# Narrow side products in the full shape of the array, and attention scores of both halves of the partitions in turns

## The chip, the cores and the metric

The kernel runs on one core of a Trainium2 chip. The metric is device time in microseconds (us) for one execution of the whole program; a lower time is better. The tensor engine (PE) multiplies, the vector engine (DVE) and the scalar engine (ACT) work on its results, GpSimd (POOL) and SyncE (SP) mainly start transfers (DMA).

## The reference

Two blocks of two layers each work on `x` of 256 tokens and 1024 channels, in float32. What the change touches is in the lines below: in the first block the retention with its normalisation by head, in the second the indexer of the sparse attention, the gates of the mLSTM, the norms of queries and keys, and the two attentions with a softmax (sparse attention over the keys that the indexer chose, and the difference of two softmax maps, weighted by lambda).

```python
# first block
o = head_groupnorm(retention_chunkwise(qh, kh, vh))
y_ret = (silu(g_ret) * o) @ w_ret_out
...
# second block: indexer and sparse attention
rel = relu(einsum('bqhd,bsd->bqhs', qi, ki))
score = einsum('bqh,bqhs->bqs', wi * idx_scale, rel)
_, idx = top_k(where(causal, score, -inf), 64)
p = softmax(einsum('bqhd,bqkhd->bhqk', q, k_sel) * dh ** -0.5)
y_b = einsum('bhqk,bqkhd->bqhd', p, v_sel)
...
# differential attention
lam_val = exp(sum(lam[0] * lam[1])) - exp(sum(lam[2] * lam[3])) + lam_init
p = softmax(einsum('bqhcd,bshcd->bhcqs', dq, dk) * d ** -0.5)
y_c = einsum('bhqs,bshv->bqhv', p[:, :, 0] - lam_val * p[:, :, 1], dv)
```

Around these stand the large products with the weights (`w_in`, the branches' matrices, the feed-forward matrices), which make up nearly all of the arithmetic.

## The kernel before

**Main products.** The weights come from memory in one stream of chunks, in the order in which PE takes them. ACT rounds each chunk to a high part `whi`, DVE forms the rest `wlo`; the activations are split in the same way (`hh` and `hl`, `yh` and `yl`). A 128x128 block of weights then meets 256 tokens in three products, `whi` with `hh`, `whi` with `hl` and `wlo` with `hh`, which add up in a PSUM tile `acc` (method `job`, through the helper `mm`, L403).

**Side products.** Everything else on PE goes to PSUM tiles named `sp`, of which there are four buffers: sums over channels by a table of constants, scores, transpositions (helper `tr`, L408), products of probabilities and values. They are written in Python generators, which `job` advances between its main products. The framework's scheduler then fixes one order for each engine, and every engine takes its own order strictly from the front. A visit, below, is a run of side products between two main products.

**Shapes of a side product.** The constants `cst` hold tables: `st4` (the mean over a head of 128 channels, one of four columns filled), `st8` (over 64 channels, eight columns), `hm2`, and `sel`, which picks the rows of `misc` that hold the mLSTM's gates. Multiplied with a table of 4 or 8 columns PE uses 4 or 8 columns of the array; with 64 rows of `misc` or with scores, whose channels are 64, half of its rows; with the gate rows `rows` four rows; with lambda (`lnl`) one row. Profile rows give this as `128*4`, `64*128`, `4*128`, `1*128`, and the full array as `128*128`. These products are in float32 and run in two passes each; the trace has one record for each pass. A transposition by `tr` has one.

**Scores.** Channels of 64 mean that a tile of 128 partitions holds two heads, or two maps, one in each half of the partitions. The work goes by groups of sets in the same half. There are two query tiles `t` of 128 tokens; tile 0 sees 128 keys, with four sets in a group, tile 1 sees 256 keys, with two. In the generator `ahead` each group is scored into one `sp` tile, masked by DVE into `prob`, its row maxima `smx` are reduced on DVE, and ACT takes the exponential with the row sums (`softmax_group`). One group is kept ahead of its use; its use is `transposed` (four transpositions of `prob` into `sp`, which ACT copies to `pt`) and a product of `pt` with the values `sv` or `dv`, into `yt`. For differential attention two maps are joined before the transposition.

**What stands ahead on the queues.** SP carries the weight stream and the rows that go to many partitions (`spread`); POOL carries exchanges of channels for the rotation (`swap`) and rows that go to DRAM (`rows`).

Of the kernel before, what the change touches and what calls it, by code (L numbers as in the profile page):

```python
# [29 lines left out]
TAKEN = -3.4e38  # L30

# [15 lines left out]
# norms after which the first chunks of weights and what they meet go unsplit  # L47
WHOLE = (1, 2, 3, 4)
# tiles of a product that ends a chain, the last ones apart
COLUMNS = ((0, 2), (2, 2), (4, 2), (6, 1), (7, 1))  # L50
# gates and products of the branches, in their order
# [8 lines left out]
def ffn_up(arr, l):  # L60
    """Gate and value tiles side by side; the first two products take four tiles."""
    t = [[_cols(i * P, P), _cols(FF + i * P, P)] for i in range(KF)]
    return [(arr, (l,), "B", KD, c) for c in [t[0] + t[1], t[2] + t[3]] + t[4:]]


def plan():
    """The weights in the order in which the tensor engine takes them: (array, index, kind,
    k tiles, columns), kind "B" by column tiles of 128 and "A" by rows of 512."""
# [104 lines left out]
def pack_params(inputs=None):  # L173
    """Per-channel parameters, channels on partitions: (offsets, array)."""
# [38 lines left out]
def make_consts():  # L213
    """Tables that depend on shapes alone: (offsets, array [128, n])."""
# [12 lines left out]

    add("ident", np.eye(P))
# [8 lines left out]
    e4 = np.zeros((P, 4, 4))  # L237
    for h in range(4):
        e4[:, h, h] = 1.0 / P
    add("st4", e4)  # L240
    s8 = np.zeros((P, 4, 8))
    for t in range(4):
        s8[:64, t, 2 * t] = 1.0 / 64
        s8[64:, t, 2 * t + 1] = 1.0 / 64
    add("st8", s8)
    hm = np.zeros((P, 2))
    hm[:64, 0] = 1.0 / 64
    hm[64:, 1] = 1.0 / 64
    add("hm2", hm)
    sel = np.zeros((P, 3, 4))  # L250
    for h in range(4):
        sel[64 + h, 0, h] = 1.0
        sel[68 + h, 1, h] = 1.0
        sel[72 + h, 2, h] = 1.0 / 16
    add("sel", sel)
# [15 lines left out]
def whole_chunks():  # L271
    """The chunks that go to the tensor engine as float32, unsplit."""
    out, n, i = set(), 0, 0
    for _, _, kind, nk, cols in plan():
        if kind == "B" and len(cols) == 4:
            if i // 2 in WHOLE:
                out.add(n // CB)
            i += 1
        n += nk * (len(cols) if kind == "B" else 4)
    return out  # L280


class Weights:
    """The stream of weights: loads ahead, then each chunk as the sum of two float32r parts."""
# [13 lines left out]
    def cuts(self, c):  # L298
        """The first chunk comes in halves."""
        return [slice(0, CW // 2), slice(CW // 2, CW)] if c == 0 else [slice(0, CW)]  # L300
# [43 lines left out]
class Gen:  # L344
# [44 lines left out]

    def p(self, name, l, i=0, n=1):  # L390
        o, m = self.poff[(name, l)]
        assert i + n <= m
        return self.prm[:, o + i:o + i + n]
# [53 lines left out]
    def split(self, hi, lo, src):  # L447
        """src as the sum of its float32r rounding and of the exact rest."""
# [3 lines left out]
    def behind(self, engine):  # L452
        """What is traced here is issued after the engine's last urgent instruction."""
# [21 lines left out]
    def side(self):  # L475
        """Steps of the tasks beside the products, as far as the vector engine keeps up."""
# [13 lines left out]
    def job(self, evac, mov, needs=(), scale=None, last=False, spare=None):  # L490
        """The next product of the plan. mov(k) gives the two parts of the activations' tile k;
        scale, per token, is for activations that were not normalised yet; spare gives tiles."""
# [3 lines left out]
        if kind == "B":  # L496
            n = len(cols)
            accs = [self.acc() for _ in range(-(-n // 2))]
            if self.idle is not None:
                # only to keep the tensor engine's clock up while it waits  # L500
# [4 lines left out]
            for k in range(nk):  # L505
                xs = mov(k)
                for t in range(n):
# [4 lines left out]
                    # a start clears the marks of its whole bank: the first product of a bank has it  # L512
# [32 lines left out]
    def swap(self, out, src):  # L545
        """src with the halves of each 64 channels exchanged"""
# [3 lines left out]
    def rows(self, r):  # L550
        # r in DRAM, from where a row goes to many partitions
# [4 lines left out]
    def spread(self, out, row):  # L556
        """a row on all the partitions of out"""
        self.nc.sync.dma_start(out, row.to_broadcast(list(out.shape)))

# [7 lines left out]
    def _lam(self, pool):  # L567
# [14 lines left out]
        ps = self.sp()  # L582
        self.mm(ps[:, 0:2], self.ones[0:1, 0:P], nl)
        self.copy(self.nlam, ps[:, 0:2])
# [6 lines left out]
    def rstd(self, pool, ps, scale, name):  # L591
        """1 / sqrt(scale * ps + eps)"""
# [6 lines left out]
    def sumsq(self, out, last, hold):  # L599
        """Over channels, on every partition: the sum of the squares of the eight tiles, which it  # L600
        takes by pairs, the last two also one by one (send). The first ones are added up before.
        With hold the tensor engine gets them together at the end."""
# [37 lines left out]
    def start_norm(self, g, l, folded=4):  # L640
        """Takes x by pairs of tiles (feed) for a norm whose scale per token comes last."""
# [20 lines left out]
    def end_norm(self, sd=None):  # L662
        """What the first products take, with their scale, and what the others take."""
# [38 lines left out]
    def branches(self, order, bufs, pool, mov, gate_load, needs, ys, done):  # L702
        """The sum over branches of gate * (branch output times its matrix), as two parts. A gate
        sigmoid(z) comes as tanh(z / 2), its double less 1."""
# [57 lines left out]
    def unscale(self, sd):  # L762
        """x out of u"""
# [10 lines left out]
    def out_proj(self, mov, g, l):  # L774
        """Four products whose columns are scaled by g, with the sum of their squares."""
# [11 lines left out]
    def first_mix(self, l, norm):  # L787
        dmov, rs, whole, mov = norm
        nc = self.nc
        with ExitStack() as st:  # L790
# [6 lines left out]
            def new_y(b):  # L797
                """Buffers for a branch's output, once those of the one before last are free."""
# [13 lines left out]
            # conformer convolution  # L812
# [65 lines left out]
            # retention  # L878
# [18 lines left out]
            def ret_a():  # L897
# [10 lines left out]
                for h in range(4):  # L908
                    ps = self.sp()
                    t, b = h // 2, (h % 2) * 64  # L910
                    q, k = rot["q"][b:b + 64, t], rot["k"][b:b + 64, t]
                    self.mm(ps[:, :T], k[:, :P], q)
                    self.mm(ps[:, T:T + P], k[:, P:], q[:, P:])
                    s = tl([P, 384], f"S{h}")
                    self.tt(s, ps[:, :384], dec[:, h], OP.mult)
                    self.S.append(s)
                    if h % 2:
                        yield
# [4 lines left out]
            # short convolution  # L923
# [33 lines left out]
            def ret_b():  # L957
# [14 lines left out]
                st4 = self.c("st4").rearrange("p (h m) -> p h m", h=4)  # L972
                for h in range(4):
                    self.mm(ps[0:4, :T], st4[:, h], sqs[h // 2][:, (h % 2) * T:(h % 2 + 1) * T],
# [82 lines left out]
    def residual(self, mov, gpre, l):  # L1057
        """x += four products; then the next norm's input."""
# [17 lines left out]
    def second_mix(self, l, norm):  # L1076
        dmov, rs, whole, mov = norm
        nc = self.nc
        with ExitStack() as st:
# [11 lines left out]
            def new_y(b):  # L1091
                """Buffers for a branch's output, once those of the one before last are free."""
# [14 lines left out]
            def rope(o):  # L1107
                """Rotates two tiles in place."""
# [6 lines left out]
            # indexer  # L1115
# [5 lines left out]
            sel = self.c("sel").rearrange("p (a b) -> p a b", a=3)  # L1121
# [5 lines left out]
            def index():  # L1127
# [9 lines left out]
                for t in range(2):  # L1137
                    self.mm(pw[:, 4 * t:4 * t + 4], misc[64:, t * P:(t + 1) * P], sel[64:, 2])
# [3 lines left out]
                for t in range(2):  # L1142
                    n = P * (t + 1)
                    rel = {}
                    for g in range(2):
                        ps = self.sp()
                        for j in range(2):
                            b = g * 64
                            self.mm(ps[:, j * n:(j + 1) * n], v3(iq)[b:b + 64, j, t * P:(t + 1) * P],
                                    ik[b:b + 64, :n])  # L1150
                        r = tmp()
# [27 lines left out]
            # key/value rank  # L1179
            ckh = pool.tile([P, 2, T], F32R, name="ckh")  # L1180
            ckl = pool.tile([P, 2, T], F32R, name="ckl")
            ck, cks = (tl([P, 512], "prob", tag="prob", bufs=4) for _ in range(2))
# [30 lines left out]
            def q_task(sqs, dst, rq):  # L1213
                """rotation of the queries, and their scale per token and head"""
                for i in range(2):
                    pq = self.sp()
                    for t in range(2):
                        for j in range(2):
                            self.mm(pq[:, 4 * j + 2 * t:4 * j + 2 * t + 2],
                                    sqs[i][:, t * T + j * P:t * T + (j + 1) * P], self.c("hm2"))  # L1220
# [8 lines left out]
            def k_task(sqs, dst):  # L1229
# [4 lines left out]
                s8 = self.c("st8").rearrange("p (t m) -> p t m", t=4)  # L1234
                for t in range(4):
                    self.mm(ps[0:8, :T], s8[:, t], sqs[t // 2][:, (t % 2) * T:(t % 2 + 1) * T],
# [17 lines left out]
            # mLSTM queries and keys  # L1254
# [29 lines left out]
            # mLSTM gates  # L1284
            def gates_task():
                ps = self.sp()
                self.mm(ps[0:4, :T], sel[64:, 0], misc[64:])
                self.mm(ps[0:4, T:], sel[64:, 1], misc[64:])
# [14 lines left out]
                idn = self.c("ident")[0:4, 0:4]  # L1303
                for t in range(2):
                    self.mm(ps[:, 4 * t:4 * t + 4], ig[:, t * P:(t + 1) * P], idn)
                    self.mm(ps[:, 8 + 4 * t:12 + 4 * t], fx[:, t * P:(t + 1) * P], idn)
# [80 lines left out]
            # attention with a softmax: sets of (queries, keys) of 64 channels  # L1387
            def softmax_group(q, k, rq, t, grp, bias, p, sums):
                """p = exp(scores - max) for the queries of tile t, sums its row sums. A group is
                sets in the same half of the partitions, one a tile."""  # L1390
                half, tiles = grp
# [243 lines left out]
```

## Time and profile before

| | us |
|---|---|
| median of three runs | 1789.97 (1788.31 to 1790.07) |
| profiled execution, first to last instruction (span) | 1789.1 |
| PE busy in the span | 1777.4 (99%) |
| DVE busy | 1363.0 (76%) |
| ACT busy | 1111.0 (62%) |
| POOL busy | 70.2 (4%) |

The profiled execution has no time of its own beside its span; the median of the runs lies 0.9 us above that span. The clock granted to PE is full in all forty slices of the page. Busy time of PE includes time in which the array fills or drains, so 99% doesn't mean that it multiplies at its peak. A change in the number or length of PE's visits shows in the time unless a wait takes its place.

### The profile page before, as it was taken

The numbers are of one execution on the slowest core, as the hardware profiler recorded it, in microseconds if no ns is written. First come the engines' busy times: TensorE is split into PE (matmuls) and PEld (weight loads), VectorE is DVE, ScalarE is ACT, GpSimd is POOL, SyncE is SP. The second block draws the span as 40 slices with busy tenths as digits, with TensorE's granted clock in tenths as the row PEclk, the third lists the DMA queues.
The fourth block names the chain that finished last, engine by engine and source line by source line (L and its number), as shares of the span: only waits on it lengthen the run. The fifth ranks groups of instructions, "written<-read, shape, count | busy, mean of one in ns | idle before, by whom it ended". The sixth has DMA issues, their size and how long they took to land.

```text
span 1789.1 us, 35765 instructions
## 1 busy us (share of the span) xinstructions
PE 1777.4 (99%) x14462; PEld 1729.2 (97%) x14462; DVE 1363.0 (76%) x2082; ACT 1111.0 (62%) x1787; POOL 70.2 (4%) x144
## 2 busy tenths in 40 slices
PE   8999999999999999999999999999999999999999
PEld 8999999999999999999998999999999999999999
DVE  8988679865999769884887877865569887677553
ACT  7575468755666567765576666654457666655542
POOL 0000000000000000000022100000000310000000
PEclk9999999999999999999999999999999999999999
DMA  7555546554655546555465644565555664356663
GB/s 265 191 171 179 187 154 200 188 187 164 210 168 188 177 138 204 189 189 188 137 195 177 201 142 139 168 207 194 189 186 180 199 201 139 124 177 200 193 196 132
DMA packets 94648, 322.52 MB, mean 180 GB/s; under 512 B 12257, under 2 KB 16913, under 8 KB 94482
## 3 DMA queue, kind: packets, MB, share of 16 engines
q1 hardware_dynamic: 91010, 314.15, 53.9%
q0 software_dynamic: 3328, 6.09, 1.1%
q8 instruction: 113, 1.85, 0.4%
q14 instruction: 53, 0.43, 0.1%
q10 hardware_dynamic: 144, 0.00, 0.0%
HBM read 312.80 MB, written 1.10 MB: 175 GB/s over the span
## 4 chain that ended last, share of the span: by engine, by line
PE 97%; DVE 1%; DMA 1%; issue 0%; ACT 0%; POOL 0%; SPq 0%; DVEq 0%; ACTq 0%; POOLq 0%
PE acc L403 90%; PE sp L403 6%; PE sp L408 1%; DMA tmp<-dq 0%; DMA Wm<-rows 0%; DMA x<-x 0%; DVE wlo L415 0%; DVE sc L1167 0%; DVE x L415 0%; DVE m L1166 0%; DVE yw L420 0%; ACT sd L445 0%; DVE dq L415 0%; ACT whi L326 0%; POOL tmp L548 0%
## 5 line engine op out<-in xcount | busy, mean ns | idle before, releaser
L326 ACT ACTIVATE whi<-wraw 128x1024 fp32r<-128x1024 f32 (+1 forms) x575 | 606.7, 1057 | 535.9 <-PE acc L403 367.8
L415 DVE TENSOR_TENSOR wlo<-wraw,whi 128x1024 fp32r<-128x1024 f32 (+1 forms) x575 | 699.0, 1220 | 282.9 <-ACT whi L326 281.3
L403 PE MATMUL acc<-hh,whi 128*128 128x256 f32 x2832 | 791.4, 280 | 0.0
L403 PE MATMUL acc<-hl,whi 128*128 128x256 f32 x2832 | 790.8, 280 | 0.0
L403 PE MATMUL acc<-hh,wlo 128*128 128x256 f32 x2832 | 789.9, 280 | 0.0
L403 PEld LDWEIGHTS acc<-hh,whi 128*128 128x128 f32 x2832 | 531.0, 188 | 5.5 <-issue 3.7
L403 PEld LDWEIGHTS acc<-hl,whi 128*128 128x128 f32 x2832 | 531.7, 188 | 1.9 <-issue 1.2
L403 PEld LDWEIGHTS acc<-hh,wlo 128*128 128x128 f32 x2832 | 531.4, 188 | 1.1 <-issue 0.8
L403 PE MATMUL acc<-yh,whi 128*128 128x256 f32 x1280 | 269.7, 284 | 6.2 <-ACT whi L326 6.2
L403 PE MATMUL acc<-yh,wlo 128*128 128x256 f32 x832 | 231.3, 283 | 0.0
L403 PEld LDWEIGHTS acc<-yh,whi 128*128 128x128 f32 x1280 | 210.5, 190 | 7.1 <-ACT whi L326 6.2
L403 PE MATMUL acc<-fh,wlo 128*128 128x256 f32 x704 | 196.0, 278 | 0.0
L403 PE MATMUL acc<-fl,whi 128*128 128x256 f32 x704 | 195.6, 278 | 0.0
L403 PE MATMUL acc<-fh,whi 128*128 128x256 f32 x704 | 195.5, 278 | 0.0
L403 PEld LDWEIGHTS acc<-yh,wlo 128*128 128x128 f32 x832 | 155.8, 189 | 0.4
L403 PEld LDWEIGHTS acc<-fh,wlo 128*128 128x128 f32 x704 | 132.3, 188 | 0.0
L403 PEld LDWEIGHTS acc<-fl,whi 128*128 128x128 f32 x704 | 132.2, 188 | 0.0
L403 PEld LDWEIGHTS acc<-fh,whi 128*128 128x128 f32 x704 | 132.0, 188 | 0.0
L403 PE MATMUL acc<-yl,whi 128*128 128x256 f32 x384 | 108.2, 282 | 0.0
L403 PEld LDWEIGHTS acc<-yl,whi 128*128 128x128 f32 x384 | 72.1, 188 | 0.2
L445 ACT ACT_TABLE_LOAD x50 | 64.2, 1283 | 5.5 <-DVE Wm L426 3.0
L420 DVE SCALAR_TENSOR_TENSOR up<-z,prm,up 128x254 f32<-128x254 f32 (+1 forms) x128 | 55.3, 479 | 0.0
(282 smaller groups left out, 1815.2 us busy)
## 6 DMA issues: line engine op xcount, KB each, us to landing
wraw<-stream SPq DMA_DIRECT2D x581, 512.0 KB, 3.6
kr<-rows SPq DMA_DIRECT2D x32, 64.0 KB, 3.0
dec<-decay SPq DMA_DIRECT2D x2, 768.0 KB, 4.3
x<-x SPq DMA_DIRECT2D x4, 256.0 KB, 6.3
rf<-rows SPq DMA_DIRECT2D x8, 128.0 KB, 3.5
tmp<-dq POOLq DMA_DIRECT2D x16, 64.0 KB, 3.8
Wm<-rows SPq DMA_DIRECT2D x8, 128.0 KB, 3.6
tmp<-dk POOLq DMA_DIRECT2D x16, 64.0 KB, 3.9
```

Source lines behind the costliest of these rows:

```text
L326: nc.scalar.activation(h[:, s], r[:, s], AF.Copy)
L403: return self.nc.tensor.matmul(out, lhsT, rhs, start=start, stop=stop, **kw)
L408: return self.nc.tensor.transpose(out, in_, self.c("ident")[:k, :k])
L415: self.recent = self.nc.vector.tensor_tensor(out=out, in0=a, in1=b, op=op)
L420: return self.nc.vector.scalar_tensor_tensor(out, a, s, b, op0=op0, op1=op1)
L445: return self.nc.scalar.activation(out, in_, f, **kw)
```

## The change

The tables `st4`, `st8` and `sel` are stored as strips of zeros with one filled column, or two, and a product takes a window of 66 columns (`SEL`) that is slid so that the filled column stands at the head's place; results other than the first 4 or 8 rows of `sp` are not read. `misc` enters with all 128 partitions. The gate rows `ig` and `fx` are transposed by `tr` instead of multiplied with a piece of the identity. `hm2` is gone: two columns of `st8` have the same numbers. Lambda goes to all partitions over DRAM, by `rows` on POOL and `spread` on SP, instead of by a product. Scores of two groups in opposite halves are issued in turns, product by product, into two `sp` tiles; in `ahead` this holds for a pair of groups, which are scored together and masked together before the softmax of the first and then of the second; `prob` and `sums` have five buffers instead of four. Comments and docstrings are removed.

```diff
+SEL = 66
...
+    e4 = np.zeros((P, 7))
+    e4[:, 3] = 1.0 / P
+    add("st4", e4)
+    s8 = np.zeros((P, 14))
+    s8[:64, 6] = 1.0 / 64
+    s8[64:, 7] = 1.0 / 64
+    add("st8", s8)
...
+    def window(self, name, i):
+        o = self.coff[name][0] + i
+        return self.cst[:, o:o + SEL]
...
-        ps = self.sp()
-        self.mm(ps[:, 0:2], self.ones[0:1, 0:P], nl)
-        self.copy(self.nlam, ps[:, 0:2])
+        self.spread(self.nlam, self.rows(nl))
...
-                    self.mm(ps[0:4, :T], st4[:, h], sqs[h // 2][:, (h % 2) * T:(h % 2 + 1) * T],
+                    self.mm(ps[:SEL, :T], self.window("st4", 3 - h), sqs[h // 2][:, (h % 2) * T:(h % 2 + 1) * T],
                             start=h == 0, stop=h == 3)
...
-                    self.mm(pw[:, 4 * t:4 * t + 4], misc[64:, t * P:(t + 1) * P], sel[64:, 2])
+                    self.mm(pw[:, 4 * t:4 * t + 4], misc[:, t * P:(t + 1) * P], sel[:, 0:4])
...
-                    self.mm(ps[0:8, :T], s8[:, t], sqs[t // 2][:, (t % 2) * T:(t % 2 + 1) * T],
+                    self.mm(ps[:SEL, :T], self.window("st8", 6 - 2 * t), sqs[t // 2][:, (t % 2) * T:(t % 2 + 1) * T],
                             start=t == 0, stop=t == 3)
...
-                self.mm(ps[0:4, :T], sel[64:, 0], misc[64:])
-                self.mm(ps[0:4, T:], sel[64:, 1], misc[64:])
+                self.mm(ps[:SEL, :T], self.window("sel", 8), misc)
+                self.mm(ps[:SEL, T:], self.window("sel", 4), misc)
...
-                    self.mm(ps[:, 4 * t:4 * t + 4], ig[:, t * P:(t + 1) * P], idn)
-                    self.mm(ps[:, 8 + 4 * t:12 + 4 * t], fx[:, t * P:(t + 1) * P], idn)
+                    self.tr(ps[:, 4 * t:4 * t + 4], ig[:, t * P:(t + 1) * P])
+                    self.tr(ps[:, 8 + 4 * t:12 + 4 * t], fx[:, t * P:(t + 1) * P])
...
+            def scores(q, k, t, pair):
+
+                n = P * (t + 1)
+                pss = [self.sp() for _ in pair]
+                for j in range(len(pair[0][1])):
+                    for ps, (half, tiles) in zip(pss, pair):
+                        i, b = tiles[j], half * 64
+                        qs, ks = v3(q[i // 2])[b:b + 64, i % 2], v3(k[i // 2])[b:b + 64, i % 2]
+                        self.mm(ps[:, j * n:(j + 1) * n], qs[:, t * P:(t + 1) * P], ks[:, :n])
+                return pss
...
+                gs, old = groups(t), None
+                for i in range(0, len(gs), 2):
+                    pair = gs[i:i + 2]
+                    new = []
+                    for grp, ps in zip(pair, scores(q, k, t, pair)):
+                        p = tl([P, 512], "prob", tag="prob", bufs=5)
+                        masked(ps, t, len(grp[1]), bias, p)
+                        new.append((grp, p, tl([P, 4], "sums", tag="sums", bufs=5)[:, :len(grp[1])]))
+                    for x in new:
+                        softmax(rq, t, *x)
+                        if old:
+                            yield old
+                        old = x
+                yield old
```

The scheduler moves the side products of the attentions among the main products. The first place is the last pair of groups of sparse attention in the first layer of the second block, on PE; `sk1`, `sq1` are keys and queries, `prob_12617` and `pt_12741` the third of the four groups of tile 1 before the change, `sp_12716` or `sp_12722` the transposed output of differential attention. Before:

```order
L408 MATMUL sp_12716<-cst_70,yt_12308 128x128 x4
L403 MATMUL sp_12727<-sk1_11860,sq1_11962 128x256 x2
L408 MATMUL sp_12736<-cst_70,prob_12617 128x128 x4
L403 MATMUL acc_13332<-hl_10522,whi_13269 128x256
...
L403 MATMUL acc_13395<-yh_12227,whi_13299 128x256
L403 MATMUL acc_13428<-yh_12227,whi_13333 128x256
L403 MATMUL sp_12775<-sv0_11899,pt_12741 128x64
```

And with the change (the same group is `prob_12623` here, the last one `prob_12626`):

```order
L409 MATMUL sp_12722<-cst_70,yt_12308 128x128 x4
L409 MATMUL sp_12736<-cst_70,prob_12623 128x128 x4
L404 MATMUL sp_12775<-sv0_11899,pt_12741 128x64
L404 MATMUL sp_12775<-sv1_11900,pt_12741 128x64
L404 MATMUL sp_12775<-sv0_11899,pt_12741 128x64
L404 MATMUL sp_12775<-sv1_11900,pt_12741 128x64
L409 MATMUL sp_12814<-cst_70,prob_12626 128x128 x4
L404 MATMUL acc_13395<-yh_12227,whi_13299 128x256
```

Between the transpositions into `sp_12736` and the product that takes their copy `pt_12741` there were 25 main products, 23 of them the rest of `acc_13332`; now there are none. In the second layer 35 main products stand at the same place.

The second place is the same stretch on ACT. Before:

```order
L445 ACTIVATE prob_12617,sums_12618<-prob_12617,smx_12623,rqs_11965 128x256 x2
L326 ACTIVATE whi_13363<-wraw_13239 128x1024
L445 ACTIVATE yd_12721<-sp_12716,prm_71 128x512
L445 ACTIVATE yh_12227<-yd_12721 128x4x128
L445 ACTIVATE pt_12741<-sp_12736 128x512
```

And with the change:

```order
L446 ACTIVATE prob_12623,sums_12625<-prob_12623,smx_12629,rqs_11965 128x256 x2
L323 ACTIVATE whi_13396<-wraw_13273 128x1024
L446 ACTIVATE prob_12626,sums_12628<-prob_12626,smx_12731,rqs_11965 128x256 x2
L446 ACTIVATE yd_12727<-sp_12722,prm_71 128x512
L446 ACTIVATE pt_12741<-sp_12736 128x512
L446 ACTIVATE yh_12227<-yd_12727 128x4x128
```

The exponentials of the pair's second group moved ahead of the copy `pt_12741`, and `yh` behind it.

## Rows read from the trace of the kernel before

**Rows 1.** The page: busy us by engine (share of the span), instructions.
```profile
PE 1777.4 (99%) x14462; PEld 1729.2 (97%) x14462; DVE 1363.0 (76%) x2082; ACT 1111.0 (62%) x1787; POOL 70.2 (4%) x144
```
**Rows 2.** Waits of the tensor engine: for whom, total us, times, longest us.
```profile
PE acc L403 <- ACT whi L326: 6.2, 1, 6.2
...
PE sp L403 <- DVE Wm L420: 0.8, 1, 0.8
```
**Rows 3.** The chain that ended last, its longest pieces: start us, us, what, how many.
```profile
251.65 177.61 PE acc L403 x1508
1150.37 166.84 PE acc L403 x1472
1613.05 172.40 PE acc L403 x1521
```
**Rows 4.** Timeline of PE, a full-shape side product: start us, us, engine, line, operation.
```profile
16.44 0.28 PE L403 MATMUL acc<-yh,wlo 128*128 128x256 f32 x1
16.56 1.03 PE L403 MATMUL sp<-sqt,ones 128*128 128x256 f32 x4
...
17.66 0.39 PE L403 MATMUL acc<-yh,wlo 128*128 128x256 f32 x2
```
**Rows 5.** Timeline of PE around the sums of `osq` in the first layer.
```profile
113.82 0.28 PE L403 MATMUL acc<-hh,wlo 128*128 128x256 f32 x1
114.03 1.89 PE L403 MATMUL sp<-osq,cst 128*4 128x256 f32 x8
...
116.07 0.28 PE L403 MATMUL acc<-hl,whi 128*128 128x256 f32 x1
```
**Rows 6.** Timeline of PE, main products before and behind lambda's one-row product.
```profile
25.02 0.28 PE L403 MATMUL acc<-yh,whi 128*128 128x256 f32 x1
...
25.77 0.28 PE L403 MATMUL acc<-yh,wlo 128*128 128x256 f32 x1
```
**Rows 7.** Timeline of SyncE's queue: the next weight load behind that product.
```profile
29.75 0.33 SPq L307 DMA_DIRECT2D wraw<-stream  x1
```
**Rows 8.** DMA issues on the page: us from issue to landing.
```profile
rows<-rr POOLq DMA_DIRECT2D x2, 4.0 KB, 1.6
```
**Rows 9.** Timeline of PE, the second block's gate rows, last layer, and the product behind.
```profile
1392.86 1.05 PE L403 MATMUL sp<-cst,rows 4*128 4x4 f32 x8
...
1394.06 0.28 PE L403 MATMUL acc<-hl,whi 128*128 128x256 f32 x1
```
**Rows 10.** Chain at 1046 to 1052 us: one transposition behind main products.
```profile
1046.92 0.11 PE sp L408
```
**Rows 11.** Timeline of PE, scores of one half alone, 256 keys.
```profile
1069.93 1.13 PE L403 MATMUL sp<-sk,sq 64*128 64x256 f32 x4
...
1071.21 0.28 PE L403 MATMUL acc<-hl,whi 128*128 128x256 f32 x1
```
**Rows 12.** Timeline of PE, scores of both halves in one visit, 256 keys.
```profile
1067.13 0.48 PE L403 MATMUL sp<-dk,dq 64*128 64x256 f32 x1
1067.14 0.48 PE L403 MATMUL sp<-sk,sq 64*128 64x256 f32 x1
...
1068.43 0.28 PE L403 MATMUL acc<-hh,whi 128*128 128x256 f32 x1
```
**Rows 13.** Timeline of ScalarE behind the softmax of a group of sparse attention.
```profile
1087.93 0.60 ACT L445 ACTIVATE prob<-prob,smx,rqs 128x256 f32<-128x256 f32 x1
...
1088.53 0.58 ACT L445 ACTIVATE prob<-prob,smx,rqs 128x256 f32<-128x256 f32 x1
...
1089.11 1.04 ACT L326 ACTIVATE whi<-wraw 128x1024 fp32r<-128x1024 f32 x1
1090.06 0.67 ACT L445 ACTIVATE yd<-sp,prm 128x512 f32<-128x512 f32 x1
...
1091.30 0.58 ACT L445 ACTIVATE pt<-sp 128x512 f32<-128x512 f32 x1
```
**Rows 14.** VectorE's masks from 1028 to 1108 us: busy us, mean ns, idle before.
```profile
L415 DVE TENSOR_TENSOR prob<-sp,mb 128x512 f32<-128x512 f32 x6 | 4.0, 687 | 1.2 <-PE sp L403 1.2
```

More of the change, by code (lines that the diff above doesn't have):

```diff
@@ L226, in add @@
         parts.append(a)
+    e4 = np.zeros((P, 7))
[5 more added lines that the diff above has]
+    add("st8", s8)
+    sel = np.zeros((P, 12))
+    for h in range(4):
+        sel[72 + h, h] = 1.0 / 16
+        sel[68 + h, 4 + h] = 1.0
+        sel[64 + h, 8 + h] = 1.0
+    add("sel", sel)
     add("ident", np.eye(P))
@@ L236, in make_consts @@
     add("causb", np.where(i[None, :] > i[:, None], NEG, 0.0))
[L237 to L255, printed above, removed]
     return off, pos, np.concatenate(parts, axis=1)
@@ L907, in ret_a @@
                 self.S = []
[L908 to L918, printed above, removed]
+                for t in range(2):
+                    pss = [self.sp() for _ in range(2)]
+                    for o, m in ((slice(0, T), slice(0, P)), (slice(T, T + P), slice(P, T))):
+                        for ps, b in zip(pss, (0, 64)):
+                            q, k = rot["q"][b:b + 64, t], rot["k"][b:b + 64, t]
+                            self.mm(ps[:, o], k[:, m], q[:, m.start:])
+                    for h, ps in zip((2 * t, 2 * t + 1), pss):
+                        s = tl([P, 384], f"S{h}")
+                        self.tt(s, ps[:, :384], dec[:, h], OP.mult)
+                        self.S.append(s)
+                    yield
             t_ra = self.spawn(ret_a())
@@ L971, in ret_b @@
                 ps = self.sp()
-                st4 = self.c("st4").rearrange("p (h m) -> p h m", h=4)
                 for h in range(4):
-                    self.mm(ps[0:4, :T], st4[:, h], sqs[h // 2][:, (h % 2) * T:(h % 2 + 1) * T],
+                    self.mm(ps[:SEL, :T], self.window("st4", 3 - h), sqs[h // 2][:, (h % 2) * T:(h % 2 + 1) * T],
                             start=h == 0, stop=h == 3)
@@ L1120, in second_mix @@
             maskb = [tl([P, P], "mb0"), tl([P, T], "mb1")]
-            sel = self.c("sel").rearrange("p (a b) -> p a b", a=3)
+            sel = self.c("sel")
             rows = tl([4, 4, T], "rows")
@@ L1144, in index @@
                     rel = {}
[L1145 to L1148, printed above, removed]
+                    pss = [self.sp() for _ in range(2)]
+                    for j in range(2):
+                        for ps, b in zip(pss, (0, 64)):
                             self.mm(ps[:, j * n:(j + 1) * n], v3(iq)[b:b + 64, j, t * P:(t + 1) * P],
                                     ik[b:b + 64, :n])
+                    for g, ps in enumerate(pss):
                         r = tmp()
@@ L1181, in second_mix @@
             ckl = pool.tile([P, 2, T], F32R, name="ckl")
-            ck, cks = (tl([P, 512], "prob", tag="prob", bufs=4) for _ in range(2))
+            ck, cks = (tl([P, 512], "prob", tag="prob", bufs=5) for _ in range(2))
             def ck_evac(a):
@@ L1219, in q_task @@
                             self.mm(pq[:, 4 * j + 2 * t:4 * j + 2 * t + 2],
-                                    sqs[i][:, t * T + j * P:t * T + (j + 1) * P], self.c("hm2"))
+                                    sqs[i][:, t * T + j * P:t * T + (j + 1) * P], self.c("st8")[:, 6:8])
                     o = rq[:, :, :, 2 * i:2 * i + 2].rearrange("p j b t -> p j t b")
@@ L1233, in k_task @@
                 ps = self.sp()
-                s8 = self.c("st8").rearrange("p (t m) -> p t m", t=4)
                 for t in range(4):
-                    self.mm(ps[0:8, :T], s8[:, t], sqs[t // 2][:, (t % 2) * T:(t % 2 + 1) * T],
+                    self.mm(ps[:SEL, :T], self.window("st8", 6 - 2 * t), sqs[t // 2][:, (t % 2) * T:(t % 2 + 1) * T],
                             start=t == 0, stop=t == 3)
@@ L1302, in gates_task @@
                 ps = self.sp()
-                idn = self.c("ident")[0:4, 0:4]
                 for t in range(2):
-                    self.mm(ps[:, 4 * t:4 * t + 4], ig[:, t * P:(t + 1) * P], idn)
-                    self.mm(ps[:, 8 + 4 * t:12 + 4 * t], fx[:, t * P:(t + 1) * P], idn)
+                    self.tr(ps[:, 4 * t:4 * t + 4], ig[:, t * P:(t + 1) * P])
+                    self.tr(ps[:, 8 + 4 * t:12 + 4 * t], fx[:, t * P:(t + 1) * P])
                 self.copy(acol, ps[:, 0:16])
@@ L1385, in mlstm, with masked @@
                         yield
-            def softmax_group(q, k, rq, t, grp, bias, p, sums):
-                half, tiles = grp
-                n, ng, b = P * (t + 1), len(tiles), half * 64
-                ps = self.sp()
-                for j, i in enumerate(tiles):
-                    qs, ks = v3(q[i // 2])[b:b + 64, i % 2], v3(k[i // 2])[b:b + 64, i % 2]
-                    self.mm(ps[:, j * n:(j + 1) * n], qs[:, t * P:(t + 1) * P], ks[:, :n])
+            def scores(q, k, t, pair):
[7 more added lines that the diff above has]
+                return pss
+            def masked(ps, t, ng, bias, p):
+                n = P * (t + 1)
                 pv, sv_ = v3(p, ng), v3(ps, ng)
@@ L1404, in softmax_group, with softmax @@
                     self.tt(pv, sv_, bias[:, None, :].to_broadcast([P, ng, n]), OP.add)
+            def softmax(rq, t, grp, p, sums):
+                half, tiles = grp
+                ng = len(tiles)
+                pv = v3(p, ng)
                 m = tl([P, 4], "smx", tag="smx", bufs=2)[:, :ng]
@@ L1433, in ahead @@
             def ahead(q, k, rq, t, bias):
-                old = None
-                for grp in groups(t) + [None]:
-                    new = None
-                    if grp:
-                        new = (grp, tl([P, 512], "prob", tag="prob", bufs=4),
-                               tl([P, 4], "sums", tag="sums", bufs=4)[:, :len(grp[1])])
-                        softmax_group(q, k, rq, t, grp, bias, *new[1:])
-                    if old:
-                        yield old
-                    old = new
+                gs, old = groups(t), None
[12 more added lines that the diff above has]
+                yield old
             def dsa():
```

## Prediction

> **What bounds the kernel now.** First the page's first part: PE is busy in 99% of the span [rows 1], DVE in 76%, ACT in 62%. Busy may hide waiting, so the list of PE's waits comes next: 6.2 us for the first chunk of weights at the start, 0.8 us for `Wm` in the middle [rows 2], and none at a group's `prob` or its copy `pt`. PE is the bound, and what its queue loses or gains shows in the time. The third view is the chain: its long pieces are main products alone, and the reader should divide. 177.61 us for 1508 is 117.8 ns each; 166.84 for 1472 and 172.40 for 1521 are 113.3 [rows 3]. So a main product has one of two paces; it changes only behind side products, and a long stretch is worth 1500 x 4.5 ns = 6.7 us. I can't tell from the trace what chooses.
>
> Last the visits. Their price is read from the timeline: start of a main product behind the visit, less that of the last one ahead of it, less 0.118 us for each main product in between. A visit of four passes in full shape gives 17.66 - 16.44 - 3 x 0.118 = 0.87, or 0.216 a pass of 256 columns [rows 4]. The sums of `osq` have eight passes in `128*4` and give 116.07 - 113.82 - 2 x 0.118 = 2.01, against 8 x 0.216 = 1.73 [rows 5]. Entering takes 0.21 instead of 0.12 us, the rest is lost behind. The shape costs some 0.29 us a visit, however long it is.
>
> **What the change gives.** *Tables.* Twelve visits become full in rows and take 66 columns: two of `osq`, six with `st8`, two each of `misc` for the indexer's weights and the gates. 12 x 0.29 = 3.4 us. No row shows 66 columns. The bounds are 0, if they count as a narrow shape like the 4 columns, and 3.5; passes cost the same 0.216 us at 4 and at 128 columns, and I take 3.4.
>
> *Lambda.* The one-row visit costs 25.77 - 25.02 - 2 x 0.118 = 0.51 us [rows 6] and goes. The two transfers in its place: rows to DRAM landed in 1.6 us [rows 8], the way back may take as long. SP waits meanwhile, and behind it stand `dec` and the weight stream, whose next load was issued only at 29.75 [rows 7], over 4 us behind the old product. This cover hides it; without it, it would be some 3 us once. I take 0.5 gained.
>
> *Gate rows.* Eight passes in the last layer cost 1394.06 - 1392.86 + 0.21 - 2 x 0.118 = 1.18 us [rows 9]. Four transpositions at 0.11 [rows 10] and 0.29 for the shape, which stays four rows, make 0.73: 0.45 gained, 0.9 in two layers. A transposition of four rows isn't in the trace; if it took as long as two passes the gain would be 0, if the shape cost nothing 1.5.
>
> *Scores.* One group of tile 1 alone costs 1071.21 - 1069.93 + 0.21 - 2 x 0.118 = 1.25 us [rows 11]. Where groups of opposite halves met in one visit their passes started 0.01 us apart, and both together cost 1068.43 - 1067.13 + 0.21 - 2 x 0.118 = 1.27 [rows 12]: the second is free. Each layer of the second block has eight such groups, six alone and two in that visit: 6 x 1.25 + 1.27 = 8.8 us. In four pairs they cost 4 x 1.27 = 5.1. That is 3.7 a layer, 7.4 in all. Tile 0, the indexer and the retention already have both halves behind one another in a visit; I take nothing there.
>
> The Trainium skill, page "TensorE: Matmul & The Clock Gate", section "The mechanism", says that matrix products never leave program order, and that small ones overlap when neighbours use different row groups. The trace disagrees in part: the visit of [rows 12] is queued as two products of one half and then two of the other, and they ran in turns. By the page the visits of tile 0 would gain as well, and the sum would be 3.5 larger; that is a rival below, priced from rows.
>
> The gains add up to 3.4 + 0.5 + 0.9 + 7.4 = 12.2 us.
>
> **What it costs.** *A copy without cover.* In the first layer of the second block the order puts the product with `pt_12741` directly behind the transpositions that it needs, where 25 main products (2.9 us) stood. On ACT, behind the exponentials that these transpositions wait for, now stand a chunk `whi`, the second group's exponentials, `yd` and only then the copy. Their durations from before, in one unbroken run of ACT: 1087.93 to 1089.11 or 1.18 for a group's exponentials, 0.95 for `whi`, 0.67 for `yd`, 0.58 for the copy [rows 13]. From the end of the first exponentials that makes 0.95 + 1.18 + 0.67 + 0.58 = 3.4 us, in which PE has four transpositions, 0.44. PE waits 3.0 us, and what stands behind it are main products that need `yh`, so nothing else can fill it. The bounds: 0.8 if ACT has all but `yd` and the copy behind it when PE arrives, 3.7 if the group is late by the second mask too (0.69 [rows 14]). I take 3.0, since that run of ACT had no gap. In the second layer 35 main products stay in between, 4.1 us, and cover the 3.4.
>
> *`Wm`.* PE waited 0.8 us there already [rows 2], at the end of a chain of DVE work and transfers that PE doesn't shorten. What PE saves shortly ahead, the gate rows' 0.45 us of that layer, comes back as waiting: 0.5.
>
> *Two masks ahead of the first maximum.* In twelve pairs the first group's maximum now stands behind the second's mask, 0.69 us [rows 14]. Whoever waits is the transposition of that group. PE waited at none of these before [rows 2], so there is some slack; the bounds are 0 and 12 x 0.69 = 8.3, and as the order keeps 31 main products (3.7 us) or more, and other visits, between a pair's scores and its first transposition, I take 0.5.
>
> **Sum.** 1789.1 - 12.2 + 3.0 + 0.5 + 0.5 = 1780.9 us of span; the median of the runs lies 0.9 above the span, so 1781.8.
>
> **Rivals.**
> - *Another pace.* Every changed visit is followed by a return to main products. The two long fast stretches [rows 3] follow sums whose surroundings keep their order, which speaks for their staying. If one falls back: 1781.8 + 6.7 = 1788.5; both, 1795. If stretches behind the `osq` visits (some 380 and 450 products) become fast, 3.7 less, and a long one 6.7 less: 1775 to 1778.
> - *No change.* Saved visits turn into waits, because the softmax chain on DVE and ACT needs its time and not PE's: what speaks against it is 76% and 62% of busy time. For this, waits must take 8 us more, which is 0.7 in each of twelve pairs: 1788 to 1791.
> - *Slower.* The same place with a larger price: if in each pair the copy or transposition waits for the second group's exponentials as in the first layer's last pair, a wait of 1.18 + 0.69 = 1.87 us in twelve pairs, 22 us, gives 1804. It decides from 1.0 us a pair, 11.7 us more than my sum. Against it: only one of the places has lost its main products.
> - *The tables stay narrow.* 66 columns count like four: 1785.2.
> - *Turns alone help.* If products of two halves need to alternate in the queue, tile 0's eight visits halve too: four passes of 0.11 [rows 10] each, 3.5 us: 1778.3. [Rows 12] speak against it.
>
> **How the numbers follow.** The sum with its smaller bounds (1778 to 1785.5) has 0.60; lower by pace, by a smaller wait or by turns, 1771 to 1778, 0.17; a long stretch slower 0.09, both 0.03; no change 0.06; slower through waits 0.05. The forecast is the first, 1781.8. For 8 in 10 the range leaves out half of the low cases and most of those above 1788: 1774.5 to 1787.5. A difference under 0.2%, 3.6 us, can't be told from none here; faster is below 1786.4, slower above 1793.5. Faster takes the first two cases and a little of the third, 0.79; same the rest of the third and no change, 0.14; slower 0.07.
>
> **What would show it.** In the changed kernel's timeline visits of `osq` have a price near 1.73, and each pair of scores at tile 1 one near 1.27 with passes 0.01 us apart. The list of waits has one for ACT's `pt` near 3.0 us in the first layer's attentions, none in the second's, and some 1.3 us for `Wm`. `rows` take one record each. The chain has two long pieces at 113.3 ns and the others at 117.8. I am wrong if waits at `prob` add up to several us, if no wait at `pt` appears, or if a long piece has another pace.

## The result, and the profile after

The changed kernel took 1803.4 us (median; 1802.6 to 1803.7) against 1790.0 of before, a ratio of 1.0074 with a 95% interval of 1.0062 to 1.0086: slower, by 13.4 us, where 8 us less was forecast. The profiled span is 1801.7 us.

The list of waits of the changed kernel, with the columns of [rows 2], shows one new entry and misses one:

```profile
PE acc L404 <- ACT whi L323: 6.7, 1, 6.7
PE sp L404 <- ACT pt L446: 2.7, 1, 2.7
PE acc L404 <- DVE yw L421: 1.0, 4, 0.3
```

The wait for the copy `pt` is the one that was forecast (2.7 us, forecast 3.0); waits at `prob` don't appear, and `Wm`, 0.8 us in [rows 2], is gone from the list. Waiting accounts for 2 us of the 13. The long pieces of the chain answer to [rows 3]:

```profile
251.15 178.45 PE acc L404 x1508
676.72 178.44 PE acc L404 x1508
1152.65 174.19 PE acc L404 x1472
1618.19 179.99 PE acc L404 x1521
```

The reader divides again: 118.33 ns a product in every one of them. The two stretches that had run at 113.3 ns lost 7.4 and 7.6 us, and those at 117.8 lost 0.8 us each. Over the whole program some 12,900 back-to-back main products take 118.33 ns in the mean, against 116.64 before: 1.69 ns x 12,900 = 22 us. No line in part 5 of the page shows this, since it gives each product 280 or 282 ns, the time from its start to its modelled end. It has to be divided out of a long piece.

The visits, meanwhile, did what they should. Timeline of PE in the changed kernel, at `osq`, at a pair of scores and at the gate rows of the last layer:

```profile
113.06 0.28 PE L404 MATMUL acc<-hh,wlo 128*128 128x256 f32 x1
113.18 1.89 PE L404 MATMUL sp<-osq,cst 128*66 128x256 f32 x8
...
115.02 0.28 PE L404 MATMUL acc<-hl,whi 128*128 128x256 f32 x1
...
1052.38 1.13 PE L404 MATMUL sp<-dk,dq 64*128 64x256 f32 x8
...
1053.67 0.28 PE L404 MATMUL acc<-hh,whi 128*128 128x256 f32 x1
...
1402.37 0.28 PE L404 MATMUL acc<-hh,wlo 128*128 128x256 f32 x1
1402.58 0.41 PE L409 MATMUL sp<-cst,rows 4*128 4x4 f32 x4
...
1403.13 0.29 PE L404 MATMUL acc<-hl,whi 128*128 128x256 f32 x1
```

`osq` enters after 0.12 us instead of 0.21 and has a price of 115.02 - 113.06 - 2 x 0.118 = 1.72 us (2.01 in [rows 5], 1.73 forecast). Two groups of scores cost 1053.67 - 1052.38 + 0.21 - 2 x 0.118 = 1.26, as forecast from [rows 12]. The gate rows cost 0.52, against 1.18 in [rows 9] and 0.73 forecast.

One more loss is not in the list of waits. Windows of the changed kernel around the wait for `pt` (the column behind POOL's is the granted clock of PE):

```profile
1078.00:1088.00 10.00, 10.00 (x86) 9.50 (x85) 5.74 (x13) 6.66 (x13) 0.00 (x0) 1.00 0.29 105
1088.00:1092.30 4.30, 1.57 (x14) 1.10 (x12) 2.65 (x6) 4.30 (x12) 0.00 (x0) 0.94 0.43 130
1092.30:1098.50 6.20, 6.20 (x29) 6.20 (x30) 0.98 (x2) 1.05 (x2) 0.00 (x0) 0.50 0.24 82
1098.50:1104.00 5.50, 5.50 (x50) 5.50 (x49) 3.31 (x5) 2.56 (x5) 0.00 (x0) 0.99 0.09 22
```

PE worked at the full clock until it waited; when it went on, 0.50 was granted for 6.2 us, which is the 1.2 GHz level. The rows there show what that costs:

```profile
1087.46 1.00 PE L404 MATMUL sp<-sv,pt 128*128 128x64 f32 x8
1088.30 0.61 PE L409 MATMUL sp<-cst,yt 128*128 128x128 f32 x4
1088.74 0.82 PE L409 MATMUL sp<-cst,prob 128*128 128x128 f32 x4
1092.29 1.97 PE L404 MATMUL sp<-sv,pt 128*128 128x64 f32 x8 [2.73 <-ACT pt L446]
1094.06 1.06 PE L409 MATMUL sp<-cst,prob 128*128 128x128 f32 x4
1094.77 0.78 PE L404 MATMUL acc<-yh,whi 128*128 128x256 f32 x2
1095.34 0.41 PE L404 MATMUL acc<-yl,whi 128*128 128x256 f32 x1
...
1098.54 0.32 PE L404 MATMUL acc<-yl,whi 128*128 128x256 f32 x1
```

Eight passes with `sv` took 1.77 us instead of 0.84, four transpositions 0.71 instead of 0.44, and 15 main products 3.20 us, 0.213 each instead of 0.118: 0.9 + 0.3 + 1.4 = 2.6 us on top of the wait. The Trainium skill, page "TensorE: Matmul & The Clock Gate", section "Why this matters for your kernels", warns that idle gaps between bursts of matrix products send the clock back to half. The trace agrees: the clock fell inside the wait of 2.73 us, as the 0.94 of the stretch with the wait and the 0.50 behind it show.

### The profile page after: what moved, and what is told of

It is laid out like the page before. It is cut to its first block, busy times and chain, and to the rows that moved or that the text cites. A ratio compares the mean times of both kernels' runs of the same rounds, so it can differ in the third digit from the quotient of the medians.

```text
span 1801.7 us, 35750 instructions
## 1 busy us (share of the span) xinstructions
PE 1787.7 (99%) x14452; PEld 1749.0 (97%) x14452; DVE 1362.7 (76%) x2081; ACT 1110.7 (62%) x1787; POOL 68.9 (4%) x145
## 4 chain that ended last, share of the span: by engine, by line
PE 99%; ACT 1%; DVE 0%; DMA 0%; issue 0%; ACTq 0%
PE acc L404 92%; PE sp L404 6%; PE sp L409 1%; DMA x<-x 0%; DVE x L416 0%; ACT prob L446 0%; DVE yw L421 0%; ACT sd L446 0%; ACT whi L323 0%; ACT L446 0%; ACT pt L446 0%; ACT yh L446 0%; ACT junk L446 0%; ACT sqt L446 0%; ACT yd L446 0%
```

## The experiments

What all main products have in common is what they read. The changed tables are 29 columns shorter (801 instead of 830), and on chip everything behind them moved by 96 bytes a partition (29 columns are 116 bytes, but all these tiles start at multiples of 32): `hh`, `hl`, `yh`, `yl`, `fh`, `fl`, which stream through the array. The weights `whi` and `wlo` lie ahead of the tables and stayed. The addresses of the built programs, modulo 512 the same for all tiles of a kind: weights 128; streamed tiles 192 before, 96 after. Theory A said that the streamed tiles suffer because they no longer start at a multiple of 64. Its rival B was what the prediction had assumed: a stretch's pace follows from the side product from which the main products return.

**Moving the tiles.** The first three kernels have columns of zeros behind the tables and nothing else; all engines' orders are those of their parent. First the changed kernel, moved by 32 bytes.

```diff
     add("causb", np.where(i[None, :] > i[:, None], NEG, 0.0))
+    add("pad", np.zeros((P, 8)))
```

> The changed kernel with eight columns of zeros behind its tables, so that all that is allocated behind them lies 32 bytes further in each partition; the orders of all engines are the same as in the changed kernel. In the changed kernel hh, hl, yh, fh start 32 bytes past a multiple of 64, before they started at a multiple. Theory A (place in memory): main products take 118.33 ns because what they stream starts off a multiple of 64. Then the paces of before return, 117.8 ns in most stretches and 113.3 in the two long ones: 12,900 products x 1.7 ns = 22 us less than the changed kernel, some 1782; with a long stretch slow 1788. Theory B (returns): the pace follows from which visit main products return from. Orders are the same, so it stays at 118.33 and 1803. Both: the wait for pt of 2.7 us and the low clock behind it stay.

It took 1822.8 us (in brackets, here and below, the ratio to the kernel before and its interval: 1.0183, 1.0167 to 1.0198), with the wait of 2.7 us for `pt` as before. The next two are the kernel before, moved by 32 and by 64 bytes (8 and 16 columns behind `sel`).

> The kernel before with eight columns of zeros behind its tables, nothing else; hh, hl, yh, fh now start 32 bytes past a multiple of 64. Orders are the same as before. Theory A: all main products at 118.33 ns, 22 us more, some 1812. Theory B: the visits are those of before, so 1790.

> The kernel before with sixteen columns of zeros, 64 bytes: hh, hl, yh, fh at a multiple of 64 again, but 64 further. Theory A: paces of 117.8 and 113.3 ns as before, 1790, or 6.7 us off it for each long stretch that takes the other pace. If any move of the buffers, and not the place against 64, were the cause, it would go to 118.33 and 1812. Theory B: 1790.

They took 1833.7 (1.0243, 1.0227 to 1.0258) and 1817.0 (1.0149, 1.0132 to 1.0166). Theory A fell with the first and the third, which are at multiples of 64 and slow; B fell with the second and third, which have the visits and orders of before. The second long stretch of the first block, 1508 products, in the chain of the first:

```profile
684.51 180.94 PE acc L405 x1508
```

of the second:

```profile
686.83 180.96 PE acc L404 x1508
```

and of the third:

```profile
681.56 178.94 PE acc L404 x1508
```

These are 120.0, 120.0 and 118.7 ns: each place has its pace, and a kernel that differs in nothing but unused zeros loses 27 to 44 us.

**The wait for `pt`.** The fourth kernel of the same series takes the place of the first and gives each group its mask directly ahead of its maximum, with four buffers.

```diff
-                        masked(ps, t, len(grp[1]), bias, p)
-                        new.append((grp, p, tl([P, 4], "sums", tag="sums", bufs=5)[:, :len(grp[1])]))
-                    for x in new:
+                        new.append((ps, (grp, p, tl([P, 4], "sums", tag="sums", bufs=4)[:, :len(grp[1])])))
+                    for ps, x in new:
+                        masked(ps, t, len(x[0][1]), bias, x[1])
                         softmax(rq, t, *x)
```

> The changed kernel with eight columns of zeros, each group's mask directly ahead of its own maximum, and four buffers of prob and sums as before. In the order that results 26 main products stand between the transpositions of the pair's first group and the product with pt_12741 (none in the changed kernel). Theory: the wait of 2.7 us for pt goes, and with it the half clock of 1092.3 to 1098.5 us, some 3 us; 5.6 us less than the changed kernel with the pad alone. With theory A some 1777, with theory B 1798. Rival: the wait goes to another copy or prob, and it takes as long as the pad alone.

1819.8 us (1.0167, 1.0152 to 1.0183), 3.0 below the first. The wait for `pt` went, but 1.4 us for `yh` came at the same place: both theory and rival were half right. The granted clock stayed at 1.00 there.

**On chip or in DRAM.** A longer array of tables also changes DRAM and its transfer. The next kernels widen the tile on chip alone:

```diff
-        self.cst = self.cpool.tile([P, nco], F32, name="cst")
+        cst = self.cpool.tile([P, nco + 24], F32, name="cst")
+        self.cst = cst[:, :nco]
```

With 24 columns the changed kernel has the addresses of before. Five buffers of `prob` don't fit there, so it has four.

> The changed kernel with the tile of the tables 24 columns wider in the on-chip memory alone (the array and its transfer stay as changed), so that all behind it lies at the addresses of before; prob and sums have four buffers, since five don't fit there, and the order then puts 22 main products between the transpositions and the product with pt_12741. Moves of 32 and 64 bytes in the last runs gave other paces, so theory A (off a multiple of 64) has fallen. Theory S (each address has its pace): at the addresses of before main products take 117.8 and 113.3 ns again, 22 us less than the changed kernel, and with the wait for pt smaller some 1778. Theory D (the array's size in DRAM, and what the transfers do by it): 118.33 or 120 ns stay, 1800 or more. Theory B (returns): any pace, but not the two of before over the same stretches.

1778.0 us (0.9931, 0.9919 to 0.9944), the value of theory S; its long pieces:

```profile
252.21 177.61 PE acc L405 x1508
676.01 177.61 PE acc L405 x1508
1144.27 166.84 PE acc L405 x1472
1601.10 172.40 PE acc L405 x1521
```

To the hundredth of a microsecond these are the pieces of [rows 3]. The same for the kernel before, wider by 8 and by 128 columns:

> The kernel before with the tile of the tables eight columns (32 bytes) wider on chip; the array in DRAM and its transfer as before, orders as before. Theory S: the same as with the longer array, 120.0 ns with gaps of 116 to 125, 1833. Theory D: 1790.

> The kernel before with the tile of the tables 128 columns (512 bytes) wider on chip, nothing else. All streamed tiles move by 512 bytes, the weights whi and wlo stay. If only the place within a period counts and 512 is a multiple of it, the paces are 117.8 and 113.3 and the time 1790; if the absolute distance to the weights counts, another pace, 1800 to 1835.

1832.4 us (1.0236, 1.0220 to 1.0252), as with the longer array, and 1790.2 (1.0002, 0.9993 to 1.0011), with 177.61, 166.84 and 172.40 us for the three pieces. The place on chip counts, not the array in DRAM, and 512 bytes more make no difference. The fourth of this series is the kernel with masks in their own place, at the addresses of before:

> The changed kernel at the addresses of before (tile of the tables 24 columns wider on chip), each group's mask directly ahead of its own maximum, four buffers of prob and sums: the edits whose visits, at 120 ns, were 12.5 us shorter in all than before. Theory S: 117.8 and 113.3 ns, and 1790 - 12.5 + 0.5 = 1778, faster than both. Theory D: 1798 or more.

1781.1 us (0.9952, 0.9940 to 0.9965), 3 us slower than with only the buffers cut: it waits 1.4 us for `yh`, which the other doesn't; the rest isn't accounted for.

**Place and order apart.** The changed kernel with four buffers and nothing else has the orders of the run at 1778.0 and the addresses of the changed kernel.

```diff
-                        p = tl([P, 512], "prob", tag="prob", bufs=5)
+                        p = tl([P, 512], "prob", tag="prob", bufs=4)
```

> The changed kernel with four buffers of prob and sums instead of five, its addresses of hh, hl, yh, fh as changed; the orders are those of the last run with four buffers, which took 1778.0 at the addresses of before. Theory: two separate costs. The place alone: 118.33 instead of 116.7 ns for 12,900 products, 21 us, so 1778.0 + 21 = 1799. The fifth buffer: the order that it gives PE costs the wait of 2.7 us and some 3 us at half the clock, so this run is 4 to 6 us below the changed kernel: 1797.5 to 1799.5. Rival: the wait costs nothing by itself, and it takes 1803.

1799.3 us (1.0051, 1.0039 to 1.0064). The 13.4 us therefore are three terms, each a difference of two kernels: the edits with four buffers, at the addresses of before, 1778.0 - 1790.0 = -12.0; the 96 bytes, at equal orders, 1799.3 - 1778.0 = +21.3; the fifth buffer, 1803.4 - 1799.3 = +4.1. The last is 1.2 us less than the 2.7 of wait and 2.6 of low clock in the trace. Half of this difference is a wait of 0.6 us for `Wm`, which the run with four buffers has again:

```profile
PE acc L404 <- ACT whi L323: 6.2, 1, 6.2
PE acc L404 <- DVE yw L421: 1.0, 4, 0.3
PE sp L404 <- DVE Wm L421: 0.6, 1, 0.6
```

**Distance or place.** In the kernel before, 32 bytes ahead of everything on chip move weights and streamed tiles together:

```diff
         self.wpool = ctx.enter_context(tc.tile_pool(name="weights", bufs=1))
+        self.wpool.tile([P, 8], F32, name="shift")
```

> The kernel before with 32 bytes ahead of everything on chip, so that the weights whi and wlo and what streams past them (hh, hl, yh, fh) move together; orders as before. Theory S1: what counts is the distance between the two, modulo 512 bytes; then 117.8 and 113.3 ns and 1790. Theory S2: the place of the streamed tiles alone counts; then 120.0 ns and 1832, as when they moved alone. Another pace: both places count.

1790.2 us (1.0001, 0.9992 to 1.0010). Moved alone the streamed tiles cost 42 us, moved with the weights nothing. So what counts is a distance between what lies ahead of the tables and what lies behind them. Main products read `whi` and `wlo` of the first and the streamed tiles of the second, and I take it for the distance between these. `wraw`, from which ACT and DVE work meanwhile, lies at the same place modulo 512 and moved with them; but in the first stretch of 1508 products in the kernel before, a product takes 117.8 ns both where ACT and DVE are busy and where neither is, so their work isn't the cause. Two further distances, on the run at 1778.0 (72 and 120 columns instead of 24):

> The run at 1778.0 us (four buffers, addresses of before) with the streamed tiles 192 bytes further: hh and the others lie 256 bytes from whi and wlo, modulo 512, instead of 64. Theories S1 and S2 have no value for this place; seen so far are 0: 120.0, 64: 116.7, 96: 120.0, 128: 118.7, -32: 118.3 ns. If half the period were the best place, 113.3 ns throughout and 1778 - 43 = 1735; if places differ without such a pattern, 1780 to 1825.

> The same run with the streamed tiles 384 bytes further, which is 64 bytes ahead of whi and wlo modulo 512 (-64). If the pace depends on the size of the distance alone, 64 in either direction, 116.7 ns and 1778; if not, one of the slower paces, 1799 to 1820.

At 256 bytes 1817.7 us (1.0154, 1.0140 to 1.0170) and 120.0 ns throughout, as at 0. At -64 it took 1752.5 (0.9792, 0.9779 to 0.9805), faster than everything before it:

```profile
249.34 170.93 PE acc L405 x1508
664.86 170.94 PE acc L405 x1508
1123.78 166.85 PE acc L405 x1472
1574.80 172.41 PE acc L405 x1521
```

All four pieces are at 113.3 to 113.4 ns. The sum had been 1778 for this one and was wrong by 25 us, in the kernel's favour: at -64 the same two paces exist as at 64, but more stretches take the faster one. Three last kernels: the one before at -64 (96 columns), and the changed one with four buffers at -96 and at 32 (112 and 16 columns).

> The kernel before with the tile of the tables 96 columns wider on chip, so that hh, hl, yh, fh lie 64 bytes ahead of whi and wlo, modulo 512; orders as before. Theory S1 (distance alone): the changed kernel with four buffers went from 1778.0 to 1752.5 by this place, so 1790.2 - 25.5 = 1765, and the change is worth 12 us at this place as at that of before. Rival: the good pace at -64 came from an order of the changed kernel; then 1780 to 1790.

> The changed kernel with four buffers, streamed tiles 96 bytes ahead of the weights (160 modulo 256). All places at odd multiples of 32 were slow so far (96: 120.0, -32: 118.3 ns); if that holds, 118 to 120 ns and 1797 to 1818. If not, 113 to 118 ns and 1735 to 1797.

> The same with the streamed tiles 32 bytes behind the weights. As for -96: slow, 118 to 120 ns and 1797 to 1818, if odd multiples of 32 are slow in general.

1757.6 us (0.9816, 0.9802 to 0.9829), 1799.8 (1.0055) and 1780.0 (0.9944). The good pace at -64 is no property of the change: the kernel before gains 32.7 us by it, 7 more than forecast. And 32 bytes, at 116.7 ns a product, are not slow, so odd multiples of 32 as a class are not the cause.

| distance of streamed tiles from weights, bytes | ns a main product | us, orders of before | us, changed, four buffers |
|---|---|---|---|
| -96 | 118.7 in long pieces, 117.3 to 120.0 in shorter ones | | 1799.8 |
| -64 | 113.3, fewer 117.8 | 1757.6 | 1752.5 |
| -32 | 118.3 | | 1799.3 |
| 0 | 120.0 | | 1822.8 (five buffers) |
| 32 | 116.7, some shorter pieces 117.8 | | 1780.0 |
| 64 | 117.8, fewer 113.3 | 1790.0 | 1778.0 |
| 96 | 120.0 | 1832.4 | |
| 128 | 118.7, two shorter pieces 120.0 | 1817.0 | |
| 256 | 120.0 | | 1817.7 |

Shorter pieces can have a pace of their own; two of -96 and one of 32 show it (120.0, 117.3 and 117.8 ns):

```profile
116.82 47.04 PE acc L405 x392
1101.84 45.76 PE acc L405 x390
```

```profile
114.68 46.17 PE acc L405 x392
```

At 64 the change is worth 12.0 us, at -64 only 5.1. Such pieces tell why. The kernel before at -64 first, then the changed one at -64:

```profile
113.67 43.18 PE acc L404 x379
480.64 28.89 PE acc L404 x253
526.81 50.66 PE acc L404 x445
1081.29 40.55 PE acc L404 x356
```

```profile
113.80 46.17 PE acc L405 x392
482.23 30.00 PE acc L405 x253
529.41 52.41 PE acc L405 x445
1075.38 45.94 PE acc L405 x390
```

In the first these take 113.8 to 114.2 ns a product, in the second 117.8 to 118.6: 6 of the 6.9 us, in four pieces; at 64 both kernels have the slower pace there. Something of theory B holds after all: where a distance has two paces, what comes ahead of a stretch has a part in which one it gets, and the changed order drew worse. What in it chooses isn't shown.

## Why the prediction was wrong

- **The step that failed** stands in its first part: a main product "has one of two paces; it changes only behind side products". On this the sum left 12,900 main products as they were, and no rival went beyond the two paces. Which paces there are depends on the distance between weights and streamed tiles; the change moved that distance from 64 to -32 bytes, and main products went to 118.33 ns in every long stretch. The missing term measured 21.3 us. The diff had it in plain sight, in two tables that became shorter and one that went.
- **The visits** were right. At the places shown a table and a pair of scores came within 0.01 us of the forecast; the gate rows gained more (0.66 us in the last layer instead of 0.45). The gain with four buffers at equal addresses was 12.0 us (10.0 to 14.5 by the interval), with a new wait of 0.7 us for `hl` at the start in it and 0.5 us less at `Wm`; the sum of the gains had been 12.2. So close a match is partly luck.
- **The wait for `pt`** came at the place and for the reason given, 2.7 us instead of 3.0. What followed it was left out: PE came back at half the clock and lost another 2.6 us by the rows. Mechanism right, term mis-sized: 3.0 in the sum, 4.1 by the run with four buffers.
- **`Wm` and the masks.** 0.5 us each were expected; neither wait is in the changed kernel's list. Slower main products aren't the reason for `Wm`: with four buffers it is 0.6 us at the same 118.33 ns, and 0.7 in the changed kernel at 120.0. In the runs that have it, it is 0.3 to 0.8 us; why the changed kernel has none stays open.
- **Lambda.** The transfer was hidden in the changed kernel, but its price was too low: issued at 22.23, it held SP until 25.71, 3.5 us and not 1.6 for the first half. In the run at 1778.0 it lasts 4.5 us and stands in the chain at the start, ahead of the 0.7 us for `hl`.
- **Rivals.** "Slower" was expected from softmax waits in twelve pairs; only one pair waited. Turns in the queue gave tile 0 nothing: its visits cost 0.84 us before and after. Where the forecast had taken nothing, they gave a little: the two visits of the retention's scores and the indexer's first went from 1.8 to 1.7 us.

## What to carry to other kernels

Ahead of counting instructions, compare the on-chip addresses of what the main loop reads: tables made 116 bytes shorter a partition cost 21.3 us by their place, where the shorter products gave 12.0. Where the tensor engine is the bound, read its pace by dividing a long piece of the chain by its products, and try a few paddings before and after a change; here 96 unused columns gave 32.7 us. And price a wait of the tensor engine with the clock that it comes back at.

## What was not expected of the hardware

- The pace of a product of 256 columns in this stream depends on the distance in bytes between its weights and its streamed operand: 113.3 to 120.0 ns, the same for 64 and 576 bytes and for 0 and 256. Why, and whether the period is 256, stays open; 160 (-96) and 128 gave the same 118.7 in long pieces, which fits no simple rule of the sizes tried.
- At 64 and at -64 there are two paces, 113.3 and 117.8 ns. A stretch keeps its pace until PE does something else; besides a visit a wait can end it: in the run with masks in their own place at the addresses of before, products went from 113.3 to 117.8 ns behind the wait of 0.8 us for `hl`. At -96, 32 and 128 some shorter stretches differ from the long ones; at -32, 0, 96 and 256 all stretches of over 100 products have one pace.
- Four transpositions of four rows cost 0.52 us among full-shape products, against 0.73 expected: entering and leaving took 0.21 and 0.22 us, 0.12 each among main products, but the four themselves 0.33, which is 0.08 each where 0.11 had been taken.
